# State-space stage of a hybrid decoder: later transposes and Toeplitz products, gelus half a period later, powers loaded from ScalarE's queue

## The chip, the cores and the metric

The kernel runs on one core of one Trainium2 chip. The metric is the time of one execution in device microseconds (us). The inputs lie in HBM as float32, laid out for the kernel on the host; the whole computation, both layers and the final norm, is one launch.

## What is computed

Two residual layers on a sequence of 512 tokens with 1024 channels. Layer 0 mixes tokens by a grouped diagonal complex state-space model (S5), layer 1 by a gated DeltaNet. The change touches layer 0 alone. Cut to what matters there:

```python
def s5_mixer(h, w_in, lam, log_dt, b, c, d_skip, w_glu, w_out):
    u, z = split(h @ w_in, 2)                  # 512 x 2048 each
    ab = exp(lam * exp(log_dt))                # complex, 128 groups x 64 states
    bb = (ab - 1) / lam * b                    # 128 x 64 x 16
    # per group: x[t] = ab * x[t-1] + bb @ u[t];  y[t] = Re(c @ x[t])
    y = scan_over_512_steps(ab, bb, c, u) + d_skip * u
    y = gelu(y)
    y = y * sigmoid(y @ w_glu)                 # 2048 x 2048
    return (y * silu(z)) @ w_out
```

## The kernel before

Every dense product is made with three matmuls of a float32 split in two parts (`mm3`, lines 91 to 94): ScalarE (ACT) rounds a tile to a high part with a copy (CAST), VectorE (DVE) subtracts it to get the low part, and TensorE (PE) multiplies high by high, high by low and low by high. `split` (line 78) does this for a slab of activations, `get_hi` and `next_lo` (lines 337 to 348) for a weight tile of 128x1024.

The stage around the change has two streams. The first is 40 **units** (`unit`, line 375). A unit is one 128x512 output of a dense product, eight steps of three matmuls. Units 0 to 7 give the second half of u, 8 to 23 give z (through a Silu on ACT), and 24 to 39 multiply the first half of the gelu'd y (`yA`, eight slabs of 128x512) by one half of the gate's weights. `fill(n)` puts the next n steps of that stream into PE's order; `unit_end` copies finished outputs out of PSUM and rounds the weights of the unit after next.

The second stream is the state space itself in 16 **steps** of 8 groups (`Step`). The sequence is folded by four, so that one step is: loads of the powers of ab (`wt`, three DMAs out of the DRAM tile `wd`), of `bB` and of u (`s5_load`); `s5_bl` on DVE makes the folded input matrices from `bB` and `wt`, and `s5_mask` on ACT masks them; `s5_v` on PE multiplies them with u; `s5_rot` and `s5_add` on DVE turn the result by the angles whose sine and cosine ACT makes (`s5_angle`, `s5_sincos`); `s5_scan` is a scan on DVE; `s5_unrot` and `s5_state` on DVE turn back; `s5_y` on PE multiplies by the output matrices that `s5_ca` (DVE) and `s5_cl` (ACT) made. Beside that the step builds a Toeplitz product for what happens inside four tokens: `s5_kin` (a small add on DVE, two masks on ACT), `s5_kt` (four transposes on PE, four copies `tl` on ACT), `s5_out` (eight matmuls on PE into the PSUM tile of `s5_y`, then copies `yb` on ACT and the store of y to DRAM as `yd`). For the first eight steps y is read back into the slabs `part[8 + k]`.

`wd` is written by `s5_params` (line 178): DVE computes the first four powers of ab, and SP stores each as it comes (line 250). All loads and stores of this stage are issued by SyncE (SP), which takes them in order.

The loop over i (lines 609 to 661) interleaves the streams. Under `tc.manual_schedule` PE and DVE run exactly in the order in which the code is written; ACT and SP are ordered by a planner that works with modelled durations and takes the ready instruction that stands earliest in the code. In iteration i the step `prev` is i - 1, `cur` is i and `nxt` is i + 1. One iteration has 16 steps of units, that is two units. Ahead of the loop stand five units (`fill(40)`), the parameters and the first step's `s5_v`. Gelus of the first eight slabs (`gelu_a`, line 350) are written in iteration 9; since ACT is the planner's, it issues each as soon as it holds its slab to be loaded. Unit 24 frees the tiles of h, and its eight steps each split one slab of `yA` beside themselves. After the loop `fill(400)` runs what is left of the units.

After the units, lines 669 to 675 load the other eight slabs of y (`yG`), gelu them and split them into `yBhi` and `yBlo`, which take the place of `yA`'s tiles; then each of 16 gate outputs is finished with that half (`glu_half`), and the output product follows.

Of the kernel before, what the change touches and what calls it, by code (L numbers as in the profile page):

```python
# [10 lines left out]
F32 = mybir.dt.float32  # L11
# [7 lines left out]
P = 128  # L19
# [22 lines left out]
def hybrid_kernel(ctx: ExitStack, tc: tile.TileContext, a, out, dbg=None):  # L42
# [314 lines left out]
    def split_y(k):  # L357
        split(part[8 + k], yA[0][:, k, :], yA[1][:, k, :])
# [3 lines left out]
    def unit_end():  # L362
# [10 lines left out]
        ends.clear()  # L373

    def unit(n):
        if n == 24:
            hB.close()
            yAp = yAx.enter_context(tc.tile_pool(name="yAp", bufs=1, side="right", reuse_waits="tile"))
            yA.extend([yAp.tile([P, 8, T], F32R, name="yAhi"), yAp.tile([P, 8, T], F32R, name="yAlo")])
            split_y(0)  # L380
        ps = psm.tile([P, T], F32, tag="mm", name="ps_mm" if n < 24 else "ps_gh")
        whi, wlo = pairs.pop(n)
        xh, xl = (hhi, hlo) if n < 24 else yA
        for k in range(KT):
            if n == 24 and k < 7:
                split_y(k + 1)
            mm3(ps, whi[:, k * P:(k + 1) * P], wlo[:, k * P:(k + 1) * P], xh[:, k, :], xl[:, k, :],
                k == 0, k == KT - 1)
            if k == 3 and lo_within[0]:
                next_lo()  # L390
            if k < KT - 1:
                yield
        ends.append((n, ps))
        if lo_within[0]:
            unit_end()
        yield
# [41 lines left out]

    def s5_load(i):
        s = steps[i]  # L440
        s.wt = s5.tile([P, 3, 256], F32, tag="wt", name="wt", bufs=1)
        for c in range(3):
            SY.dma_start(s.wt[:, c, :], wd[c].rearrange("j g q n -> (j g) (q n)")[:, 256 * i:256 * i + 256]
                         .unsqueeze(1).to_broadcast([8, 16, 256]))
# [18 lines left out]
    def s5_sincos(s):  # L463
# [3 lines left out]
        S.activation(out=s.kr, in_=s.tau, func=AF.Abs)  # L467
        S.activation(out=s.tc, in_=s.kr, func=AF.Sin, scale=-TWO_PI_LO, bias=hpi_c)

# [122 lines left out]
    get_hi(1)  # L592
    fill(40)
    s5_params()
    s5_quad(0)
    cur = s5_load(0)
    s5_quad_b(0)
# [11 lines left out]
    with tc.manual_schedule(engines={mybir.EngineType.PE, mybir.EngineType.DVE}):  # L609
        for i in range(17):  # L610
            nxt = s5_load(i + 1) if i < 15 else None
            if i in (1, 5, 9):
                s5_quad((i + 3) // 4)
            if prev:
                s5_y(prev)
            if cur:
                s5_rot(cur)
            fill(3)
            if prev:
                s5_kin(prev)  # L620
            if cur:
                s5_add(cur)
                s5_cl(cur)
            fill(1)
            next_lo()
            if prev:
                s5_kt(prev)
            if i == 9:
                gelu_a(range(8))
            if nxt:  # L630
                s5_frac(nxt)
                s5_bl(nxt)
            fill(2)
            if nxt:
# [3 lines left out]
            fill(2)  # L638
            unit_end()
            if prev:  # L640
                s5_out(prev)
            if cur:
                s5_unrot(cur)
            fill(4)
            if nxt:
                s5_sincos(nxt)
                s5_side(nxt)
            if i < 14:
                s5_angle(steps[i + 2])
            if nxt:  # L650
                s5_v(nxt)
# [3 lines left out]
            if nxt:  # L655
                s5_ca(nxt)
            if i in (1, 5, 9):
                s5_quad_b((i + 3) // 4)
            fill(4)
            unit_end()  # L660
            prev, cur = cur, nxt
# [10 lines left out]
    yBlo = yBp.tile([P, 8, T], F32R, name="yBlo")  # L672
    with tc.tile_pool(name="yGp", bufs=1, reuse_waits="tile") as yGp:
        for k in range(8):
            split(load_gelu(8 + k, yGp.tile([P, T], F32, name=f"yG{k}")), yBhi[:, k, :], yBlo[:, k, :])
    def glu_half(m, hf, ps, yh, yl):
# [692 lines left out]
```

## Time and profile before

| | us |
|---|---|
| median of three runs | 1084.86 |
| lowest and highest | 1084.20 and 1087.56 |
| the profiled execution, its own time | 1086.08 |
| span of that execution's trace | 1084.4 |

The profile is of that one execution. Busy times of an engine are sums over its instructions; a matmul's end is modelled, so that what PE really loses is better seen from the starts of its instructions and from its waits. All times in a trace are us from the start of its span. An engine that stands idle is charged to what released it. The bracket at the end of a row gives the idle time ahead of that instruction and the releaser.

### The profile page before, as it was taken

How to read it: one execution, taken by the hardware profiler on the slowest of the kernel's cores; microseconds unless marked ns; L12 is line 12 of the kernel's file. 1: busy time of each engine (PE TensorE's matmuls, PEld its weight loads, DVE VectorE, ACT ScalarE, POOL GpSimd, SP SyncE). 2: the span in 40 equal slices, each digit the busy share in tenths (PEclk: the TensorE clock that was granted, in tenths of full speed). 3: DMA queues.
4: the chain of work that ended last, by engine and by line, in shares of the span. 5: the costliest groups of instructions: out<-in, count | busy, mean ns of one | idle time of the engine just before them, and what ended most of it. 6: DMA issues, size and time to landing. Idle time of an engine off the chain costs nothing. (4 is left out here: it accounts for less than half of the span.)

```text
span 1084.4 us, 15225 instructions
## 1 busy us (share of the span) xinstructions
PE 1041.8 (96%) x5620; PEld 869.5 (80%) x5620; DVE 774.9 (71%) x1246; ACT 599.8 (55%) x1163; POOL 57.5 (5%) x62
## 2 busy tenths in 40 slices
PE   7999999998999989999999999999999999999997
PEld 5887878886888868878899777778888888887887
DVE  5994999998999838666785688679951444556253
ACT  4573799989787564334446566733343655424241
POOL 0100000000000000000001004310020000200000
PEclk9999999998999999999999999999999999999999
DMA  8776666675354268866751342132241001123342
GB/s 300 265 244 200 192 195 197 190 214 168 99 148 126 91 248 313 299 208 225 251 179 57 111 164 78 59 99 96 104 131 60 20 20 39 59 72 110 100 146 78
DMA packets 85628, 161.42 MB, mean 149 GB/s; under 512 B 10417, under 2 KB 44593, under 8 KB 85554
## 3 DMA queue, kind: packets, MB, share of 16 engines
q1 hardware_dynamic: 84546, 157.31, 45.0%
q0 software_dynamic: 1008, 3.15, 1.1%
q8 instruction: 44, 0.72, 0.3%
q14 instruction: 30, 0.25, 0.1%
HBM read 141.67 MB, written 18.74 MB: 148 GB/s over the span
## 5 line engine op out<-in xcount | busy, mean ns | idle before, releaser
L79 ACT CAST whi<-wraw 128x1024 fp32r<-128x1024 f32 (+1 forms) x101 | 99.1, 981 | 175.8 <-PE ps_mm L93 74.9
L80 DVE TENSOR_TENSOR wlo<-wraw,whi 128x1024 fp32r<-128x1024 f32 (+1 forms) x101 | 116.1, 1149 | 92.9 <-ACT whi L79 79.6
L92 PE MATMUL ps_mm<-g_hhi,whi 128*128 128x512 f32 x360 | 148.3, 412 | 0.4 <-ACT whi L79 0.4
L93 PE MATMUL ps_mm<-g_hlo,whi 128*128 128x512 f32 x360 | 147.0, 408 | 0.0
L94 PE MATMUL ps_mm<-g_hhi,wlo 128*128 128x512 f32 x360 | 145.8, 405 | 0.5 <-DVE wlo L80 0.5
L94 PEld LDWEIGHTS ps_mm<-g_hhi,wlo 128*128 128x128 f32 x360 | 67.7, 188 | 14.7 <-DVE wlo L80 1.0
L92 PE MATMUL ps_mm<-hhi,whi 128*128 128x512 f32 x192 | 79.3, 413 | 0.0
L92 PEld LDWEIGHTS ps_mm<-g_hhi,whi 128*128 128x128 f32 x360 | 67.7, 188 | 14.3 <-ACT whi L79 0.8
L93 PEld LDWEIGHTS ps_mm<-g_hlo,whi 128*128 128x128 f32 x360 | 67.8, 188 | 12.6
L94 PE MATMUL ps_mm<-hhi,wlo 128*128 128x512 f32 x192 | 75.8, 395 | 0.0
L93 PE MATMUL ps_mm<-hlo,whi 128*128 128x512 f32 x192 | 75.5, 393 | 0.0
L857 DVE SCALAR_TENSOR_TENSOR ac<-ps_mm,cw,ac 128x509 f32<-128x509 f32 (+2 forms) x87 | 64.7, 744 | 3.6 <-ACT ac L854 2.9
L103 DVE SCALAR_TENSOR_TENSOR adaw<-adaw,cact 128x1024 f32<-128x1024 f32 x48 | 58.8, 1228 | 5.0 <-DMA adaw<-in_adaw_dram 4.9
L92 PE MATMUL ps_gh<-yAhi,whi 128*128 128x512 f32 x128 | 53.8, 420 | 3.6 <-ACT yAhi L79 3.6
L346 DVE TENSOR_TENSOR wlo<-wraw,whi 128x1024 fp32r<-128x1024 f32 x40 | 48.7, 1219 | 10.8 <-ACT whi L340 10.8
L340 ACT CAST whi<-wraw 128x1024 fp32r<-128x1024 f32 x40 | 41.8, 1044 | 24.2 <-issue 7.7
L93 PE MATMUL ps_gh<-yAlo,whi 128*128 128x512 f32 x128 | 51.2, 400 | 1.1 <-DVE yAlo L80 1.1
L94 PE MATMUL ps_g<-yBhi,wlo 128*128 128x512 f32 x128 | 50.1, 391 | 1.4 <-DVE wlo L80 1.4
L93 PE MATMUL ps_g<-yBlo,whi 128*128 128x512 f32 x128 | 50.2, 393 | 1.1 <-DVE yBlo L80 1.1
L92 PE MATMUL ps_g<-yBhi,whi 128*128 128x512 f32 x128 | 50.1, 391 | 1.2 <-ACT yBhi L79 1.2
L94 PE MATMUL ps_gh<-yAhi,wlo 128*128 128x512 f32 x128 | 51.0, 399 | 0.0
L94 PEld LDWEIGHTS ps_mm<-hhi,wlo 128*128 128x128 f32 x192 | 36.4, 190 | 8.2
(343 smaller groups left out, 2535.8 us busy)
## 6 DMA issues: line engine op xcount, KB each, us to landing
adaw<-in_adaw_dram SPq DMA_DIRECT2D x48, 512.0 KB
wraw<-in_wginb_dram SPq DMA_DIRECT2D x45, 512.0 KB
wraw<-in_wglu_dram SPq DMA_DIRECT2D x32, 512.0 KB
wraw<-in_winb_dram SPq DMA_DIRECT2D x24, 512.0 KB
bB<-in_bB_dram SPq DMA_DIRECT2D x16, 384.0 KB
wt<-wd SPq DMA_DIRECT2D x48, 128.0 KB
wraw<-in_s5o_a_dram SPq DMA_DIRECT2D x16, 384.0 KB
wraw<-in_wgo_a_dram SPq DMA_DIRECT2D x16, 384.0 KB
```

The costliest lines, as they stand in the source:

```text
L79: S.copy(hi, src)
L80: V.tensor_tensor(out=lo, in0=src, in1=hi.bitcast(F32), op=ALU.subtract)
L92: TE.matmul(ps, whi, xhi, start=start, stop=False)
L93: TE.matmul(ps, whi, xlo, start=False, stop=False)
L94: TE.matmul(ps, wlo, xhi, start=False, stop=stop)
L103: return V.scalar_tensor_tensor(out=aw, in0=aw, scalar=1.0, in1=cact, op0=ALU.mult, op1=ALU.mult, accum_out=mods[:, n:n + 1]).ins
L340: S.copy(pairs[n][0], raws[n])
L346: V.tensor_tensor(out=lo, in0=raws.pop(n), in1=hi.bitcast(F32), op=ALU.subtract)
L857: V.scalar_tensor_tensor(out=ac[:, d:], in0=ps[:, 0:T - d], scalar=cw[:, n, k:k + 1], in1=ac[:, d:], op0=ALU.mult, op1=ALU.add)
```

## The change

- The powers of the first step are loaded by three DMAs that ACT issues and no longer SP. The other steps keep SP.
- Four units and no longer five stand ahead of the loop (`fill(32)`). One unit more is left for the end.
- Within an iteration the transposes (`s5_kt`) move from behind the fourth step of units to behind the sixth, and the Toeplitz products (`s5_out`) from behind the eighth to behind the tenth. `s5_y`, `s5_v` and `unit_end` stay where they are, at 0, 12, 8 and 16 steps.
- The gelus of the first eight slabs are queued on ACT behind the sine and cosine of step 10 (in iteration 9). `s5_v` of that step moves to the end of iteration 9, ahead of unit 24, which now begins with iteration 10. The first two slabs of `yA` are split at the end of iteration 9, the other six beside the first three steps of unit 24.
- The loads for the last four steps' tables (`s5_quad`, `s5_quad_b`) move from iteration 9 to 10, and in iteration 10 the small add of `s5_kin` stands ahead of the first units.
- After the units, the loads and gelus of the other eight slabs are written in a loop of their own with a higher priority for the planner, and the splits follow in a second loop.

```diff
--- before.py
+++ after.py
@@ -372,18 +372,21 @@
             get_hi(n + 2)
         ends.clear()
 
+    def start_half():
+        hB.close()
+        yAp = yAx.enter_context(tc.tile_pool(name="yAp", bufs=1, side="right", reuse_waits="tile"))
+        yA.extend([yAp.tile([P, 8, T], F32R, name="yAhi"), yAp.tile([P, 8, T], F32R, name="yAlo")])
+        split_y(0)
+        split_y(1)
+
     def unit(n):
-        if n == 24:
-            hB.close()
-            yAp = yAx.enter_context(tc.tile_pool(name="yAp", bufs=1, side="right", reuse_waits="tile"))
-            yA.extend([yAp.tile([P, 8, T], F32R, name="yAhi"), yAp.tile([P, 8, T], F32R, name="yAlo")])
-            split_y(0)
         ps = psm.tile([P, T], F32, tag="mm", name="ps_mm" if n < 24 else "ps_gh")
         whi, wlo = pairs.pop(n)
         xh, xl = (hhi, hlo) if n < 24 else yA
         for k in range(KT):
-            if n == 24 and k < 7:
-                split_y(k + 1)
+            if n == 24 and k < 3:
+                split_y(2 * k + 2)
+                split_y(2 * k + 3)
             mm3(ps, whi[:, k * P:(k + 1) * P], wlo[:, k * P:(k + 1) * P], xh[:, k, :], xl[:, k, :],
                 k == 0, k == KT - 1)
             if k == 3 and lo_within[0]:
@@ -436,11 +439,11 @@
                         in1=qT[:, 2:3, ns].unsqueeze(3).to_broadcast([P, 2, 16, 16]), op=ALU.mult)
         V.tensor_tensor(out=bb, in0=ys[0], in1=ys[1], op=ALU.subtract)
 
-    def s5_load(i):
+    def s5_load(i, q=SY):
         s = steps[i]
         s.wt = s5.tile([P, 3, 256], F32, tag="wt", name="wt", bufs=1)
         for c in range(3):
-            SY.dma_start(s.wt[:, c, :], wd[c].rearrange("j g q n -> (j g) (q n)")[:, 256 * i:256 * i + 256]
+            q.dma_start(s.wt[:, c, :], wd[c].rearrange("j g q n -> (j g) (q n)")[:, 256 * i:256 * i + 256]
                          .unsqueeze(1).to_broadcast([8, 16, 256]))
         s.bB = s5.tile([P, 3, 256], F32, tag="bB", name="bB")
         SY.dma_start(s.bB, a["bB"].rearrange("p (c n) -> p c n", c=3)[:, :, 256 * i:256 * i + 256])
@@ -465,7 +468,7 @@
         s.ts = s5.tile([P, 4, P], F32, tag="tsin", name="tsin")
         S.activation(out=s.ts, in_=s.tau, func=AF.Sin, scale=-TWO_PI_LO)
         S.activation(out=s.kr, in_=s.tau, func=AF.Abs)
-        S.activation(out=s.tc, in_=s.kr, func=AF.Sin, scale=-TWO_PI_LO, bias=hpi_c)
+        return S.activation(out=s.tc, in_=s.kr, func=AF.Sin, scale=-TWO_PI_LO, bias=hpi_c).ins
 
     def s5_side(s):
         qs = slice(4 * s.i, 4 * s.i + 4)
@@ -590,10 +593,10 @@
     get_hi(0)
     next_lo()
     get_hi(1)
-    fill(40)
+    fill(32)
     s5_params()
     s5_quad(0)
-    cur = s5_load(0)
+    cur = s5_load(0, S)
     s5_quad_b(0)
     s5_bl(cur)
     s5_mask(cur)
@@ -609,54 +612,60 @@
     with tc.manual_schedule(engines={mybir.EngineType.PE, mybir.EngineType.DVE}):
         for i in range(17):
             nxt = s5_load(i + 1) if i < 15 else None
-            if i in (1, 5, 9):
+            if i in (1, 5, 10):
                 s5_quad((i + 3) // 4)
             if prev:
                 s5_y(prev)
             if cur:
                 s5_rot(cur)
+            if prev and i == 10:
+                s5_kin(prev)
             fill(3)
-            if prev:
+            if prev and i != 10:
                 s5_kin(prev)
             if cur:
                 s5_add(cur)
                 s5_cl(cur)
-            fill(1)
             next_lo()
-            if prev:
-                s5_kt(prev)
-            if i == 9:
-                gelu_a(range(8))
             if nxt:
                 s5_frac(nxt)
                 s5_bl(nxt)
-            fill(2)
+            fill(3)
+            if prev:
+                s5_kt(prev)
             if nxt:
                 s5_mask(nxt)
             if cur:
                 s5_scan(cur)
             fill(2)
             unit_end()
+            fill(2)
             if prev:
                 s5_out(prev)
             if cur:
                 s5_unrot(cur)
-            fill(4)
+            fill(2)
             if nxt:
-                s5_sincos(nxt)
+                last = s5_sincos(nxt)
                 s5_side(nxt)
+            if i == 9:
+                with tc.issue_after(last):
+                    gelu_a(range(8))
             if i < 14:
                 s5_angle(steps[i + 2])
-            if nxt:
+            if nxt and i != 9:
                 s5_v(nxt)
             if cur:
                 s5_state(cur)
             next_lo()
             if nxt:
                 s5_ca(nxt)
-            if i in (1, 5, 9):
+            if i in (1, 5, 10):
                 s5_quad_b((i + 3) // 4)
             fill(4)
+            if i == 9:
+                s5_v(nxt)
+                start_half()
             unit_end()
             prev, cur = cur, nxt
         lo_within[0] = True
@@ -671,8 +680,13 @@
     yBhi = yBp.tile([P, 8, T], F32R, name="yBhi")
     yBlo = yBp.tile([P, 8, T], F32R, name="yBlo")
     with tc.tile_pool(name="yGp", bufs=1, reuse_waits="tile") as yGp:
+        yG = []
         for k in range(8):
-            split(load_gelu(8 + k, yGp.tile([P, T], F32, name=f"yG{k}")), yBhi[:, k, :], yBlo[:, k, :])
+            with tc.high_priority(600):
+                yG.append(load_gelu(8 + k, yGp.tile([P, T], F32, name=f"yG{k}")))
+        for k in range(8):
+            split(yG[k], yBhi[:, k, :], yBlo[:, k, :])
+
     def glu_half(m, hf, ps, yh, yl):
         whi, wlo = load_w(a["wglu"][2 * m + hf])
         for k in range(8):
```

## Rows read from the trace of the kernel before

**Rows 1.** Page, part 1: busy us (share of span) and instructions.
```profile
PE 1041.8 (96%) x5620; PEld 869.5 (80%) x5620; DVE 774.9 (71%) x1246; ACT 599.8 (55%) x1163; POOL 57.5 (5%) x62
```

**Rows 2.** Waits of PE, 66 to 362 us: total, times, longest.
```profile
PE ps_kt L566 <- ACT kin L560: 4.4, 4, 2.3
PE ps_y L574 <- ACT tl L569: 3.8, 4, 1.8
PE ps_v L514 <- ACT bl L487: 3.6, 2, 2.6
PE ps_gh L92 <- ACT yAhi L79: 3.6, 1, 3.6
```

**Rows 3.** Windows: length, busy PE, PEld, DVE, ACT, POOL; clock, DMA.
```profile
66.50:93.70 27.20, 27.20 (x121) 22.33 (x119) 18.53 (x52) 13.47 (x24) 0.00 (x0) 1.00 0.75 237
99.90:253.00 153.10, 143.68 (x790) 121.29 (x790) 150.76 (x194) 132.34 (x242) 0.00 (x0) 0.99 0.67 198
...
279.00:362.10 83.10, 82.81 (x469) 71.01 (x468) 81.63 (x106) 61.11 (x122) 0.00 (x0) 1.00 0.43 121
...
395.80:407.00 11.20, 8.36 (x30) 5.13 (x30) 8.69 (x14) 10.16 (x19) 0.00 (x0) 1.00 0.86 326
```

**Rows 4.** Waits of DVE, 99 to 362.1 us.
```profile
DVE za L523 <- PE ps_v L514: 4.9, 1, 4.9
DVE kc L558 <- PE ps_y L550: 3.0, 4, 1.3
DVE yAlo L80 <- ACT yAhi L79: 0.5, 1, 0.5
```

**Rows 5.** Timeline of DVE: start, us; first rotation of steps 0, 14 and 15.
```profile
99.94 1.23 DVE L523 TENSOR_TENSOR za<-ps_v,tcos 128x1024 f32<-128x1024 f32 x1 [4.89 <-PE ps_v L514]
...
345.65 1.22 DVE L523 TENSOR_TENSOR za<-ps_v,tcos 128x1024 f32<-128x1024 f32 x1
...
362.13 1.22 DVE L523 TENSOR_TENSOR za<-ps_v,tcos 128x1024 f32<-128x1024 f32 x1
```

**Rows 6.** Timeline of PE: v of step 0 (first matmuls) and step 15.
```profile
96.47 0.65 PE L514 MATMUL ps_v<-U,bl 128*128 128x128 f32 x3 [2.59 <-ACT bl L487]
...
357.19 1.95 PE L514 MATMUL ps_v<-U,bl 128*128 128x128 f32 x16
```

**Rows 7.** Timeline of SP's issues, 81 to 87 us.
```profile
81.64 0.86 SPq L250 DMA_DIRECT2D wd<-p  x2
82.59 0.68 SPq L443 DMA_DIRECT2D wt<-wd  x1
...
85.10 0.61 SPq L443 DMA_DIRECT2D wt<-wd  x1
...
86.26 0.43 SPq L75 DMA_DIRECT2D wraw<-in_winb_dram  x1
86.78 0.60 SPq L443 DMA_DIRECT2D wt<-wd  x1
```

**Rows 8.** Timeline of DVE, 86 to 94 us: first readers of the powers.
```profile
86.59 0.69 DVE L479 TENSOR_TENSOR ta<-bB,wt 128x512 f32<-128x512 f32 x1 [1.07 <-DMA wt<-wd]
...
93.63 0.69 DVE L480 TENSOR_TENSOR tb<-bB,wt 128x512 f32<-128x512 f32 x1 [3.02 <-DMA wt<-wd]
```

**Rows 9.** Groups of ACT, 100 to 280 us: table loads ahead of gelus.
```profile
L352 ACT ACT_TABLE_LOAD x8 | 10.3, 1283 | 0.1
```

**Rows 10.** Timeline of ACT, 351 to 358 us: iteration 14.
```profile
351.16 0.63 ACT L466 ACTIVATE tsin<-tau 128x512 f32<-128x512 f32 x1 [1.45 <-DVE tau L461]
351.70 1.69 ACT L569 COPY tl<-ps_kt 32x512 f32<-32x512 f32 x4
...
357.26 0.74 ACT L468 ACTIVATE tcos<-kr,cols 128x512 f32<-128x512 f32 x1
```

**Rows 11.** Timeline of ACT, 393 to 394.4 us: two gelus of 128x512.
```profile
393.13 1.15 ACT L585 ACTIVATE yG<-yG 128x512 f32<-128x512 f32 x2
```

**Rows 12.** Waits of PE, 395 to 407 us.
```profile
PE ps_g L92 <- ACT yBhi L79: 1.2, 1, 1.2
```

## The prediction

> **What bounds the kernel now.** I read the page first: PE is busy for 96% of the span, DVE for 71% [rows 1]. That reads as a kernel bound by PE, in which a wait of PE that goes is time won. The waits of PE in the state-space stage name what the change aims at: 4.4 us for the masked `kin` ahead of the transposes, 3.8 for the `tl` copies ahead of the Toeplitz products, 3.6 for `bl` ahead of `s5_v`, 3.6 for the first slab of `yA` [rows 2]. But a share over the whole span mixes stages, so the windows came next. From 99.9 to 253.0 us DVE is busy for 150.76 of 153.10 us, and from 279.0 to 362.1 for 81.63 of 83.10 [rows 3]. In the loop it is DVE that never rests. The waits of DVE confirm it: in 262 us it waits 3.0 us for `ps_y` and 0.5 for the split of `yA`; the 4.9 for `ps_v` lie ahead of its first rotation at 99.94 [rows 4, 5]. One period late in the loop, from rotation 14 to rotation 15, is 362.13 - 345.65 = 16.48 us [rows 5].
>
> So the loop from rotation 0 to rotation 15 lasts 262.2 us, of which 262.2 - 3.5 = 258.7 are work of DVE that the change neither adds to nor takes from. PE's work in a period is a little less, so PE falls idle now and then wherever its order first meets something that DVE has not begun yet: a kin, a tl (which waits behind a sine on ACT that waits for DVE's `tau` [rows 10]), a state. Most of the waits in [rows 2] are this lag becoming visible. Moving PE's instruction later hides the wait there and shows it elsewhere. The reader is to see that the end of the stage is: the start of rotation 0, plus DVE's loop, minus what PE may run ahead of DVE at the end, plus PE's work after that.
>
> **The change part by part.** I work out the four terms of that sum, against the profiled execution (1086.08 us, span 1084.4; 1.2 us above the median).
>
> Start of the loop. A unit is 24 matmuls; 121 of them take 27.20 us [rows 3], 0.225 each, 5.4 us a unit. With four units ahead, PE reaches the first `s5_v` 5.4 us earlier than now, near 88, and does that unit after the loop, where nothing hides it: +5.4. In return `s5_v` has to come earlier. It starts at 96.47 [rows 6]; its last input is the third power load, which DVE's reader took at 93.63 [rows 8], 2.84 us before. SP issued the three loads at 82.59, 85.10 and 86.78, the last behind a 512 KB weight load at 86.26 [rows 7]. The second waited for the stores of the powers, the last two of which began at 81.64 [rows 7]: no queue can start it before 85.10. On ACT, the second and third start at 85.10 and 85.71. The first load took 4.0 us from its issue to its reader (82.59 to 86.59), the third 6.85 (86.78 to 93.63) [rows 7, 8]. A load that ACT issues is not in this trace, so I bound it: 3.0 us as a floor (a store, at the second of the two, from about 82.07 to its reader at 85.10), 6.85 as the ceiling. I take 4.0, the load with no weights right ahead of it, as ACT's queue has none: landed at 89.7, `s5_v` at 92.55, 3.9 us earlier than now. Net +1.5 (bounds +0.5 and +4.4). ACT's issues themselves hold it for three times 0.6 us; it is busy for 13.47 of 27.20 us there [rows 3], so I cost them at nothing; without that cover they would push a weight cast by 1.8 us, and PE is waiting then anyway.
>
> DVE's idle time inside the loop, 3.5 us now. The wait for `ps_y` goes, as it comes from PE being held up by ACT in iterations 7 to 9: each early gelu brings a table load of 1.28 us, eight of them [rows 9], and one back, and waits for its slab, ahead of the `tl` copies. Behind the sine and cosine one load serves all eight. In their place comes one block: in iteration 14 the last cosine starts at 357.26 and takes 0.74, so ends at 358.0, 4.1 us before DVE is through (362.13) [rows 5, 10]; the later Toeplitz product moves both by the same. From there ACT needs 1.28 for the table, 8 gelus at 1.15 / 2 [rows 11] = 4.6, and 0.6 for the first cast, of a gelu's size: 6.5. DVE, which is to subtract next, idles 2.4. That is -1.1 (bounds: 0 idle, -3.5; and 6.2 idle, +2.7, if ACT also serves another table load, 1.28, a Silu like a gelu, 0.6, and some 2 us of weight cast and kin before the third slab).
>
> How far PE may run ahead. Now `s5_v` of step 15 starts at 357.19 and its rotation at 362.13, 4.94 later [rows 5, 6]. The limit is the `tl` chain; both it and the product that needs it move by two steps, six matmuls, 1.36 us. So the lag at the end may grow by that: -1.4 (bounds 0, if the state for the next `s5_y` binds at once, and -2.0). This is all that the shift of transposes and products brings, however many waits it hides.
>
> The second half of y. From 395.8 to 407.0 PE has 30 matmuls in 11.20 us, worth 6.8 [rows 3]: 4.4 lost while ACT alternates gelus and casts. With the gelus done early, what stays is the first cast, which can't start before unit 39 has read the tile it overwrites, 1.2 [rows 12], and the first subtraction, near 0.6, half of a 1.22 us operation on twice the columns [rows 5]: -2.6 (bounds -3.4 and 0, where the loads come too late). The work that hides the gelus is the unit left for the end.
>
> Sum: +1.5 - 1.1 - 1.4 - 2.6 = -3.6. The profiled execution would take 1082.5; set against the median, 1084.86 - 3.6 = **1081.3 us**. Nothing after 407 us changes.
>
> **The rivals.**
>
> (A) The second queue saves only issue time. The third load then still needs its 6.85 us, from 85.71: `s5_v` at 95.4, the shift costs +4.4, the sum is -0.7 and the time 1084.2. For it: DMA was busy 75% of the time just before, at 237 GB/s [rows 3], and the first load may have been quick because it was alone. Against it: the third stood right behind 512 KB on the same queue [rows 7]. The Trainium skill, in "DMA: Bandwidth & Descriptors", section "Issuing engines are not separate DMA queues", says that starting DMAs from several engines saves only the sequencer's time to start them, since all run on the same 16 engines; by that rule this rival holds. The same page, section "Queues, rings and completion order", has each DMA engine take turns between queues, by which a load on another queue need not sit out the 512 KB; no row here shows two hardware queues at once.
>
> (B) Slower: ACT reaches its three triggers late. ACT takes them in order, and where the planner puts them behind the cast that waits for the end of the fourth unit, near 88 (66.5 and four units of 5.4), they start near 89.9 with that cast and its copy done (an estimate: three gelus of 0.57 [rows 11], by their columns), the third 1.2 later, and it lands at 95.1, `s5_v` at 98; with the slow 6.85 at 100.8. The shift then costs +6.9 to +9.7 and the sum is +1.8 to +4.6, 1086.7 to 1089.5. From `s5_v` at 96.2 on the kernel is no faster than before, from 99.5 on it is slower by 0.3%. For it: the planner's modelled time need not be the chip's. Against it: on SP it put the first loads near 82.6 and 85, in good time [rows 7].
>
> (C) The waits are real. Every wait of [rows 2] and the 1.2 of [rows 12] go, 16.6 us: 1068.3. Against it stands DVE's 258.7 us of work, which would have to begin 14.5 us earlier (the 16.6, less the 3.5, 1.4 and 2.6 that the other terms can give, plus the unit's 5.4) [rows 4, 5].
>
> (D) The block of gelus costs its ceiling of 6.2 us of DVE's time, the rest as forecast: +3.8, so 1085.1. For it: casts, Silu and copies all meet there.
>
> **How the numbers follow.** The forecast has 0.53, A 0.22, B 0.13, C 0.03, D 0.09. The range takes in A and D and most of B, and the better bounds of each term (-0.9 at the start, -2.4 of idle, -0.6 of lag, -0.8 at the second half; two of the larger together): 1076 to 1088. A measurement of this kernel can tell 0.3%, 3.3 us, from no change. The forecast lies just past that: of its 0.53 some 0.43 fall beyond it, with C and a share of the early landings of A's kind 0.50 in all; within it 0.36, from the rest of the forecast, A and D; slower 0.14, B and the worst of D.
>
> **What would show it.** In the changed profile: DVE busy for 98% from rotation 0 to 15 and the period still 16.5 us; rotation 0 near 96 and not 94 or 100; `s5_v` of step 0 with a longer wait than 2.59; one gelu table load in the loop and a DVE wait for `yAhi` of some 2.4 us; rotation 15 some 6.3 us after the start of its `s5_v`; PE waits for kin and tl that shrink early and come back, at y, tl or kt, late in the loop; ps_g with one wait of 1.2. Wrong would be a period below 16.4, a first power load on ACT that takes over 6 us, or PE with no waits in the loop at all.

## The result, and the profile after

The changed kernel takes **1097.58 us** (median of 6 runs, 1093.12 to 1098.42) against 1084.53 for the kernel before on the same chip (6 runs): a ratio of **1.0097** with a 95% interval of 1.0075 to 1.0120 (the quotient of the two medians, 1.0120, is the upper end of that interval). Forecast were 1081.3 us and, with a chance of 0.14, a slower kernel. The profiled execution took 1093.12 us with a span of 1091.4, the quickest of the six; against the profiled execution of before it is 7.0 us longer.

The first part of the page of the changed kernel (busy us, share of the span, instructions):

```profile
PE 1045.0 (96%) x5620; PEld 871.9 (80%) x5620; DVE 774.4 (71%) x1246; ACT 583.1 (53%) x1148; POOL 57.6 (5%) x62
```

The shares are those of before [rows 1]: ACT has lost 15 instructions and 16.7 us. All 15 are table loads: one gelu load in the loop where there were eight [rows 9], and eight fewer of the other tables. The kernel is no faster for it. The waits of PE in the changed kernel, from 66 to 362 us (total, times, longest):

```profile
PE ps_v L517 <- ACT bl L490: 10.3, 9, 4.0
PE ps_gh L92 <- ACT yAhi L79: 3.6, 2, 2.3
PE ps_kt L569 <- ACT kin L563: 2.3, 2, 1.6
PE ps_y L577 <- ACT tl L572: 2.0, 3, 0.9
```

The waits for kin and tl have halved, as the change meant, and the wait for `bl` has grown from 3.6 to 10.3 [rows 2]: the sum went from 15.4 to 18.2 us. A wait that is only a sign of an engine behind moves when the instruction is moved. The stretches that answer to [rows 3] (length, busy PE, PEld, DVE, ACT, POOL; clock, DMA) and the waits of DVE inside the loop:

```profile
98.90:252.00 153.10, 144.93 (x808) 122.89 (x807) 151.39 (x194) 115.00 (x226) 0.00 (x0) 0.99 0.65 200
278.00:361.40 83.40, 80.44 (x449) 68.70 (x448) 82.50 (x107) 63.02 (x125) 0.00 (x0) 0.98 0.43 120
...
DVE yAlo L80 <- ACT yAhi L79: 4.2, 4, 3.1
```

DVE is busy for 99% of both stretches and now has a single cause of waiting. Its 3.0 us for `ps_y` [rows 4] are gone, 3.7 more for the split of `yA` have come. The timeline of DVE (start, us) at rotations 0, 14 and 15, and of PE at `s5_v` of steps 0 and 15:

```profile
98.95 1.23 DVE L526 TENSOR_TENSOR za<-ps_v,tcos 128x1024 f32<-128x1024 f32 x1 [5.24 <-PE ps_v L517]
344.92 1.22 DVE L526 TENSOR_TENSOR za<-ps_v,tcos 128x1024 f32<-128x1024 f32 x1
361.40 1.22 DVE L526 TENSOR_TENSOR za<-ps_v,tcos 128x1024 f32<-128x1024 f32 x1
...
95.13 0.58 PE L517 MATMUL ps_v<-U,bl 128*128 128x128 f32 x1 [4.04 <-ACT bl L490]
355.10 1.16 PE L517 MATMUL ps_v<-U,bl 128*128 128x128 f32 x9
```

Against [rows 5, 6]: rotation 0 comes 1.0 earlier, the loop lasts 262.45 in place of 262.19, the period is 16.48 in both, and the lag from `s5_v` of step 15 to its rotation grew from 4.94 to 6.30.

The table follows these marks (us, starts of single instructions) through all kernels of this study. "Units" is the last product of unit 39, "out" the first of the output projection, "solves" the stretch from the first small matmul of the first layer's solves (`ps_m`) to the product that follows them (`ps_pq`); the last column is the time against before, run on the same chip in the same set, with its interval. before-2 is the kernel before once more.

| kernel | v(0) | rot 0 | rot 15 | lag | units | units to out | solves | ratio |
|---|---|---|---|---|---|---|---|---|
| before | 96.47 | 99.94 | 362.13 | 4.94 | 395.53 | 15.92 | 56.8 | 1 |
| before-2 | 95.58 | 97.66 | 360.23 | 4.93 | 393.64 | 15.94 | 56.7 | 1.0003 (0.9988 to 1.0018) |
| **after** | 95.13 | 98.95 | 361.40 | 6.30 | 398.88 | 16.46 | 59.7 | 1.0097 (1.0075 to 1.0120) |
| a1 | 95.89 | 99.36 | 361.80 | 6.30 | 399.28 | 17.64 | 59.7 | 1.0071 (1.0043 to 1.0099) |
| b2 | 95.80 | 99.62 | 360.05 | 4.93 | 398.89 | 13.08 | 61.3 | 1.0024 (1.0002 to 1.0045) |
| b3 | 96.34 | 99.84 | 361.14 | 4.96 | 394.52 | 15.93 | 56.7 | 1.0009 (0.9996 to 1.0023) |
| b4 | 94.86 | 96.95 | 359.85 | 5.02 | 393.20 | 18.54 | 61.3 | 1.0052 (1.0030 to 1.0073) |
| b5 | 95.14 | 97.23 | 358.99 | 4.97 | 397.80 | 13.60 | 56.7 | 1.0023 (1.0004 to 1.0041) |
| c1 | 96.65 | 100.33 | 360.06 | 3.96 | 394.44 | 15.95 | 61.3 | 1.0005 (0.9985 to 1.0024) |
| a2 | 94.89 | 98.71 | 361.11 | 6.29 | 398.62 | 14.82 | 59.7 | 1.0047 (1.0031 to 1.0063) |
| a3 | 96.50 | 100.32 | 362.72 | 4.94 | 401.56 | 15.40 | 59.7 | 1.0070 (1.0049 to 1.0091) |
| a4 | 94.97 | 98.37 | 357.78 | 6.30 | 395.29 | 18.26 | 59.7 | 1.0062 (1.0038 to 1.0086) |
| d1 | 94.77 | 96.86 | 361.97 | 4.94 | 395.36 | 16.25 | 59.8 | 1.0029 (1.0014 to 1.0044) |
| d2 | 96.25 | 100.07 | 362.49 | 6.30 | 399.99 | 14.96 | 56.7 | 1.0076 (1.0047 to 1.0106) |

Of the 7.0 us of the profiled executions, 3.35 are there when the units end, 3.9 when the output projection begins, 4.3 when the solves begin, and 7.2 behind them. One pair of traces is a thin base, since the start of the loop differs by 2.3 us between before and before-2. The means of two traces each (before and before-2, after and a1) put the changed kernel 4.5 us behind at the end of the units, 5.6 at the output projection, 6.5 at the start of the solves and 9.4 behind them.

### The profile page after: what moved, and what is told of

Same layout as the page of the kernel before. It is cut to its first block, busy times and chain, and to the rows that moved or that the text cites. A ratio compares the mean times of both kernels' runs of the same rounds, so it can differ in the third digit from the quotient of the medians.

```text
span 1091.4 us, 15229 instructions
## 1 busy us (share of the span) xinstructions
PE 1045.0 (96%) x5620; PEld 871.9 (80%) x5620; DVE 774.4 (71%) x1246; ACT 583.1 (53%) x1148; POOL 57.6 (5%) x62
## 5 line engine op out<-in xcount | busy, mean ns | idle before, releaser
L80 DVE TENSOR_TENSOR wlo<-wraw,whi 128x1024 fp32r<-128x1024 f32 (+1 forms) x101 | 116.1, 1150 | 94.8 <-ACT whi L79 81.6
```

The source lines that it names most:

```text
L80: V.tensor_tensor(out=lo, in0=src, in1=hi.bitcast(F32), op=ALU.subtract)
```

## The experiments

**The changed kernel again (a1).** No edit.

> The changed kernel unaltered, for its spread and a second trace. Theory 1 (the loss lies in the state-space stage: one unit of 5.4 us more behind a loop that is bound by VectorE and starts only 1.0 us earlier): the first matmul of the second half of the gate product comes some 4 us later than before, in every trace. Theory 2 (the loss is mostly the clock): TensorE's granted clock falls below 0.97 between 830 and 840 us, in the triangular solves of layer 1, for some 3 us, and this run repeats that and shows at which other place the time goes up to the median of 1097.6.

Ratio 1.0071; together with the first measurement the change costs some 0.7 to 1.0%. The marks up to the units repeat: loop 262.44, lag 6.30, units at 399.28. The solves take 59.7 us again. So both theories have their mark, and what is lost is lost in the same places, with 1.2 us more from the units to the output projection, at a granted clock of 0.90 there (1.00 in the first trace).

**One unit less ahead, and the loads on ACT's queue (b2), in the kernel before.**

```diff
-    fill(40)
+    fill(32)
-    cur = s5_load(0)
+    cur = s5_load(0, S)
```
(with `q.dma_start` for the three loads of `s5_load`, as in the change)

> The kernel before with four units ahead of the loop and the first step's powers on ScalarE's queue, nothing else. Theory 1: the unit costs 5.4 us and the start of the loop gives back 1.0 to 1.3, so +4.1 to +4.4 at the first matmul of the second half, and the whole kernel +4 to +5. Theory 2: the same +4 there, and the clock in layer 1 decides the rest: +4 where it doesn't fall, +7 where it does. Rival (the two parts are harmless, the gelus and the shift cost the time): within 1 us.

The units end at 398.89, 3.4 later than before: PE's tail from `s5_v` of step 15 to there is 43.78 us against 38.34, one unit (5.44). Ahead of the loop next to nothing came back: rotation 0 at 99.62 is 0.3 earlier than in before and 2.0 later than in before-2; the loop itself is 1.8 shorter (260.43). But the output projection begins 13.08 after that and not 15.92, at 411.97 against 411.45. The unit covers the gelus of the second half, by 2.8 us. In this kernel, without the rest of the change, the term that I had put at -2.6 is there. The whole kernel loses some 2.6 us (1.0024), less than theory 1 had.

**The queue alone (b3).** The same edit of `s5_load`, with `fill(40)`.

> Before, with one part of the change alone: the three power loads of step 0 go on ScalarE's queue; the number of units ahead of the state-space stage stays as in before. Theory (the loads come about 1 us earlier by the issue alone, their flight hardly changes): first s5_v at 95.1 to 95.5, rotation 0 near 98.9, the last product of the units about 1.0 earlier, near 394.5, and a time 1 us below the one of before, so between 0.998 and 1.000 of it. Rival (the second queue removes the transfer behind the weights): first s5_v near 92.6, rotation 0 near 96, the end 3.5 us earlier.

Neither time came. `s5_v` starts at 96.34. The issues of ACT and the first readers of the loads on DVE in this kernel (the second row holds the second and third issue, the third row the third alone, from a window of the timeline that begins between them):

```profile
81.85 1.17 ACTq L443 DMA_DIRECT2D wt<-wd  x1
...
84.78 1.29 ACTq L443 DMA_DIRECT2D wt<-wd  x2
...
85.49 0.58 ACTq L443 DMA_DIRECT2D wt<-wd  x1
...
86.88 0.69 DVE L479 TENSOR_TENSOR ta<-bB,wt 128x512 f32<-128x512 f32 x1 [1.45 <-DMA wt<-wd]
93.50 0.69 DVE L480 TENSOR_TENSOR tb<-bB,wt 128x512 f32<-128x512 f32 x1 [5.93 <-DMA wt<-wd]
```

The third load started 1.3 us earlier than in before (85.49 against 86.78) and its reader ran 0.13 earlier (93.50 against 93.63): 8.0 us from issue to reader in place of 6.85 [rows 7, 8]. The ratio is 1.0009, with 1 in its interval: no gain. In d1, which has the same edit, the third load took 6.7 us.

**One unit of work more (b5), in the kernel before.** The 24 products of unit 39 are made twice, the first pass overwritten; nothing is left out.

```diff
+        for k in range(8 if n == 39 else 0):
+            mm3(ps, whi[:, k * P:(k + 1) * P], wlo[:, k * P:(k + 1) * P], xh[:, k, :], xl[:, k, :],
+                k == 0, k == 8 - 1)
         for k in range(KT):
```

> The kernel before with the 24 matmuls of its last unit made twice (the first pass is overwritten), so that all that follows is 5.4 us later and nothing else is changed. Theory 1: +5.4 at the first matmul of the second half, and no more after it. Theory 2: +5.4 there, and the clock may fall in the solves of layer 1 at some 830 us, since they begin at another moment: then +8 to +9 at the end.

The tail is 43.78, again 5.44 longer, and the output projection begins 13.60 after it: the second half hides 2.3 of the 5.4. Started at 97.23, near the 97.66 of before-2, it reaches the output projection at 411.40 against 409.58. So a unit of work more costs less than its length in this kernel, but not nothing.

**The shift of transposes and products alone (b4), in the kernel before.**

```diff
-            fill(1)
             next_lo()
-            if prev:
-                s5_kt(prev)
...
-            fill(2)
+            fill(3)
+            if prev:
+                s5_kt(prev)
...
             unit_end()
+            fill(2)
             if prev:
                 s5_out(prev)
             if cur:
                 s5_unrot(cur)
-            fill(4)
+            fill(2)
```

> The kernel before with the transposes and the Toeplitz products two steps later, nothing else. Theory 1 with the lag of the prediction: rotation 15 comes 6.3 us after the start of its matmuls in place of 4.94, so the end of the units 1.4 us earlier; the kernel -1.4. Rival (the waits hidden are time won): the waits for kin and tl, 8.2 us, go and the kernel is 5 us or more faster.

Neither time came: the kernel is slower, by 0.5%. The lag stayed at 5.02. One row of the windows, from 340 to 358 us, first of this kernel and then of the changed one, bears on why:

```profile
340.00:358.00 18.00, 17.92 (x101) 15.22 (x100) 17.83 (x24) 12.41 (x24) 0.00 (x0) 1.00 0.31 91
```
```profile
340.00:358.00 18.00, 17.47 (x99) 14.88 (x98) 17.79 (x24) 13.30 (x27) 0.00 (x0) 1.00 0.36 100
```

Here PE is busy without a gap (17.92 of 18.00), so a later product gives it nothing to run ahead into. In the changed kernel it waits now and then, so it is as far ahead as the order lets it be. That is how I read the two rows; no run tests it by itself. The shift alone also puts the last Toeplitz product, and with it the last store of y, 1.4 us nearer to the end of the units (10.2 ahead of it in place of 11.6). The first cast of the second half then holds PE for 4.4 us, and the output projection begins 18.54 after the units. Part of that is the clock, which falls behind this wait:

```profile
393.20:411.70 18.50, 14.14 (x50) 10.85 (x49) 12.73 (x20) 14.92 (x25) 0.00 (x0) 0.82 0.91 327
```

At 0.82, a fifth of the stretch is lost (18.5 x 0.18 = 3.3 us).

**The change without its shift (a3).** `s5_kt` and `s5_out` back at their places of before.

> The changed kernel with the transposes and Toeplitz products where they were before. Theory 1 (the shift lets TensorE run 1.36 us further ahead of VectorE): rotation 15 comes 4.94 us after the start of its matmuls in place of 6.30, the units end 1.4 us later, the last store of y is 1.4 us earlier against their end; on the whole within 1.5 us of the changed kernel. Rival (the shift costs time by itself, as the kernel before with the shift alone was 5 us slower): 3 to 5 us faster than the changed kernel.

The lag is 4.94: in the changed kernel the shift is what makes it 6.30. With that the units end 1.36 later relative to rotation 15 (38.84 against 37.48). From there to the output projection it is 15.40 against 16.46, at a granted clock of 0.89 in that stretch (1.00 in the changed kernel), which is worth some 1.7 us of it. So what the shift wins at the end of the loop it pays back right behind. The ratio, 1.0070, is that of a1, as theory 1 had it.

**The change with the second half of y written as before (a2).** One loop of load, gelu and split, no raised priority.

> The changed kernel with the loads, gelus and splits of the second half in one loop again and no raised priority, as before the change. Theory 1b (the new order of that part costs time: the loads stand behind a weight load on SyncE's queue that waits for VectorE, and ScalarE makes all eight gelus before the first cast): from the last matmul of the units to the first of the layer's first projection of layer 1 it takes 180.4 us as with the kernel before plus fill(32) and ScalarE's queue (180.36), in place of 183.8; the kernel is 3.4 us faster than the changed one. Rival (order there makes no difference): within 1 us of the changed kernel.

From the units to the output projection 14.82 us in place of 16.46, both at a granted clock of 1.00, and the ratio falls to 1.0047, below the interval of the first measurement but inside that of a1. Up to that mark the new loop loses 1.6 us. At the mark that the expectation named, the first product of layer 1's first projection, nothing of it is left in the trace: 184.05 us from the units to there, 183.81 in the changed kernel, where 180.4 was forecast. The stretch of the output projection took 1.9 us longer in this trace (169.23 against 167.35), for which I have no cause.

**The change with the early gelus free to go when the planner likes (a4).**

```diff
-                with tc.issue_after(last):
-                    gelu_a(range(8))
+                gelu_a(range(8))
```

> The changed kernel with the gelus of the first eight slabs not queued behind the sine and cosine of step 10, so that the planner places them. Theory 1 (VectorE's 258 us of work bound the loop, and table loads on ScalarE cost only what they make VectorE wait): eight table loads of 1.28 us for gelus come back, VectorE's waits for yAhi (4.2 us) shrink to 1, and the time from rotation 0 to rotation 15 stays between 259 and 262.5 us. Rival (the waits of TensorE for tl are time won by the block): the loop gets 3 us or more longer.

The loop takes 259.41 us, 3.0 less, and DVE waits 1.4 for `yAlo` and not 4.2:

```profile
DVE yAlo L80 <- ACT yAhi L79: 1.4, 2, 1.0
```

So the block of gelus behind the cosine costs 3 us of DVE's time, as theory 1 had it. The units end 3.6 earlier than in the changed kernel. Half of that was gone when the output projection began (413.55 against 415.34), since that stretch took 18.26 us, with PE waiting 3.1 for the first cast and 1.5 for a weight, and at a granted clock of 0.91. A ratio of 1.0062 can't be told from the 1.0071 of a1.

**A little less work for DVE (c1), in the kernel before.** One subtraction of each step, 0.69 us, goes to GpSimd.

```diff
-        V.tensor_tensor(out=xs, in0=xs, in1=xt, op=ALU.subtract)
+        G.tensor_tensor(out=xs, in0=xs, in1=xt, op=ALU.subtract)
```

> The kernel before with one operation a step, the last subtraction of the output matrices (128x512, 0.69 us on VectorE), on GpSimd. Theory 1 (VectorE bounds the loop): each period gets 0.6 us shorter, 15 of them 9 us, until TensorE's own work of some 16.2 us a period binds; the end of the units 5 to 9 us earlier, the kernel 5 to 9 us faster. Rival (TensorE's waits are latencies of its own): the period stays at 16.4 or more and the time within 2 us. Second rival (GpSimd and VectorE slow each other down): VectorE's operations beside it take longer than the 0.68 to 1.22 us of before.

The loop shortens by 2.5 us, not by the 9 that 15 times 0.6 would give. Three early periods lose the whole 0.7 (15.70 to 15.76 us, 16.43 to 16.48 in before), others grow, and the last four are 16.06 to 16.32. PE's waits do not vanish, and DVE now waits for PE (from rotation 0 to 15):

```profile
DVE kc L558 <- PE ps_y L550: 5.0, 11, 0.8
```

Late in the loop PE's own work stands 0.2 to 0.4 us a period behind DVE's. The second rival falls: DVE's other operations keep their 0.68 to 1.22 us beside GpSimd's 1.33. That DVE bounds the loop was right; that it alone does was not.

**The kernel before again (b0).** No edit.

> The kernel before, unaltered, for a second trace of it. Theory: the fall of the granted clock during the solves of the first layer (56.8 us in the trace of before, 59.7 in the changed kernel, 61.3 in three variants) belongs to the execution, not to the code: then this trace may show 59 to 62 us between the start of the solves and the step after them, with everything up to there within 1 us of the first trace, and a longer span by as much. Rival: it belongs to the kernel, and this trace shows 56.8 again. Time 1084 to 1088 either way; first s5_v near 96.5, rotation 0 near 99.9, the last product of the units at 395.5.

56.7 us for the solves again, as the rival had it, and a rotation 0 at 97.66: the start of the loop varies by 2.3 us between two executions of the same kernel.

**The loads of the second half on GpSimd's queue (d1, before with b3's edit; d2, the changed kernel).**

```diff
-        SY.dma_start(yr, yd[k])
+        G.dma_start(yr, yd[k])
```
(in `load_gelu`)

> Before, with the power loads of step 0 on ScalarE's queue and the eight loads of the second half of y on GpSimd's queue (idle there) in place of SyncE's. Theory: these eight loads wait on SyncE's queue behind a weight load whose buffer is not free, not for their own data; on GpSimd's queue they start by 11 us before the last product of the units (7.0 before it in the kernel before), the gelus follow earlier, and the output projection begins about 13 us after that product in place of 15.9: with the queue at the start 3 to 4 us in all, so 0.996 to 0.998 of before. Rival: the loads are bound by the landing of the last store of y, or GpSimd issues them more slowly than SyncE does: then they land no earlier and the output projection stays at 15 to 16 us after the product; time 0.998 to 1.002 of before.

> The changed kernel with the eight loads of the second half of y on GpSimd's queue. Theory: the part of the prediction that failed here (2.6 us were to be won in the second half of y) failed through the place of these loads behind a weight load on SyncE's queue; on a queue of their own they start 12 us or more before the last product of the units (7.9 in the changed kernel), all gelus are done by its end, and the output projection begins 13 to 14 us after it in place of 16.5: 2.5 to 3.4 us less than the changed kernel, so a ratio to before near 1.004 to 1.006. Rival: what binds there is the order of the work on ScalarE and VectorE (casts, subtractions, the weights of the next unit); then the loads come earlier and the output projection stays at 16 to 17.5 us after the product.

In d1 the loads start early, and nothing follows from it. GpSimd's issues, the first six of the eight, and ACT's rows some 30 us later show the reason:

```profile
361.92 3.42 POOL L584 DMA_DIRECT2D yG<-yd  x6 [302.45 <-DMA yd<-yb]
...
392.54 1.28 ACT L724 ACT_TABLE_LOAD   x1 [0.88 <-DMA yr<-yd]
393.84 0.63 ACT L724 ACTIVATE yr<-yr 128x512 f32<-128x512 f32 x1
394.37 1.14 ACT L585 ACTIVATE yG<-yG 128x512 f32<-128x512 f32 x2
```

In before, SP issues all eight from 388.53 on. But ACT takes another gelu first and waits for that one's load, so the first gelu of `yG` runs at 394.37, 1.24 later than in before [rows 11], and gelus and casts alternate as they did. The output projection begins 16.25 after the units, at a granted clock of 0.90 there (1.00 in before), so that this figure alone decides nothing. The casts do: the first starts 0.9 behind the last product of the units and the eighth 7.67, in before 0.9 and 7.69. The theory fell: in before it is the order of ACT's work that binds, not the place of the loads. In d2, where all gelus are written ahead of the casts, earlier loads do help: the first gelus start 7.84 before the last product of the units in place of 2.39, PE's wait of 1.8 for the next unit's weight goes, and the output projection begins 14.96 after it, 1.5 earlier. The wait for the first cast stays (2.8). Against before d2 is at 1.0076, not better than the changed kernel by anything that can be measured.

## Why the prediction was wrong

The frame held. Start of rotation 0, DVE's loop, the lag and PE's tail add up to the end of the units, and on to the output projection, in every kernel of the table. Up to that projection I had forecast -3.6 us; it was +3.9 (5.6 by the means of two traces each). Term by term, for the profiled pair:

**Start of the loop: forecast +1.5, measured +4.5.** This step and the second half of y failed most, by some 3 us each. The unit that is no longer ahead came back in the tail as 5.44 us, the 5.4 of [rows 3]. `s5_v` came 1.34 earlier and not 3.9, and rotation 0 came 0.99 earlier. Even that is within what the start varies by. Over the table, `s5_v` starts at 95.7 on average with five units ahead (seven traces, 94.8 to 96.6) and at 95.6 with four (seven, 94.9 to 96.5): the change gave back nothing there. Rotation 0 comes 0.9 later with four units (99.3 against 98.4), and PE's wait ahead of `s5_v`, longer with four, is followed by a clock of 0.50 to 0.58 in all seven of those traces and in three of the others (the last section has the figures). By these means the start costs 5.4 + 0.9 = 6.3. ACT issued on time. The issues on ACT in the changed kernel, and the readers:

```profile
82.76 1.17 ACTq L446 DMA_DIRECT2D wt<-wd  x1
85.49 1.29 ACTq L446 DMA_DIRECT2D wt<-wd  x2
...
87.81 0.69 DVE L482 TENSOR_TENSOR ta<-bB,wt 128x512 f32<-128x512 f32 x1 [1.48 <-DMA wt<-wd]
92.29 0.69 DVE L483 TENSOR_TENSOR tb<-bB,wt 128x512 f32<-128x512 f32 x1 [3.79 <-DMA wt<-wd]
```

I had taken 4.0 us from issue to reader. The first took 5.05. The third, issued at about 86.2 (0.71 behind the second, as in b3), took 6.1, and in b3 8.0: a queue without weights ahead of it did not make it short. Over all traces the third load took 5.5 to 6.9 us from SP's queue (five traces) and 6.1 to 8.0 from ACT's (nine), and its reader ran at 92.9 and 92.8 on average. This is close to rival A. That its `s5_v` at 95.4 and its +4.4 for the start (its own working gives +4.3) agree with the profiled trace (95.13 and +4.45) is in part luck: the trace that the forecast was made from started late, and A's gain of 1.1 us is not there on average. Between 4.0 and 6.85 I had chosen the better end, on the ground that the slow load stood behind 512 KB on its queue; that ground was wrong.

What the third load waited for stands in the DMA packets. ACT's loads ride a hardware queue of their own (q10), 136 packets each. In the changed kernel the 272 packets of the first two end at 89.80 us. Those of the third, issued at 86.2, run from 89.90 to 91.82, and its reader starts 0.5 later. The two queues from 89.85 to 92 us (packets, MB, share of 16 engines; q1 is SP's):

```profile
q1 hardware_dynamic: 335, 0.38, 49.3%
q10 hardware_dynamic: 136, 0.13, 17.3%
```

So 3.7 of the 6.1 us passed until the second load was through, with SP's data moving beside it, and 1.9 were its own transfer. In the other eight traces with ACT's queue the third load's packets, counted in order, begin within 0.5 us of the end of the second's. My 4.0 us were those of a load with none of the three ahead of it; the second load, 0.6 ahead on the same queue, stood in my sum at nothing. No run gave the three loads different queues.

The Trainium skill, "DMA: Bandwidth & Descriptors", section "Issuing engines are not separate DMA queues", says that a second issuing engine saves only the time to start the transfers. The traces here agree that no more than that is saved: the third load's reader ran 1.3 us earlier in the changed kernel and 0.1 in b3, and on average over all traces 0.1.

**DVE's idle time in the loop: forecast -1.1, measured +0.3.** The wait for `ps_y` went, as forecast, but not for my reason. It is gone in a4 too, where the eight gelu loads are back; and in before 2.1 of its 3.0 us stand in iteration 9 (256.6 to 257.6 us), the rest in 5 and 10. What a3, a4 and the changed kernel share, and before, b2 and b4 lack, is the new order around iterations 9 and 10, with unit 24 begun later; no run tests that alone. (I had also left out 0.3 us that DVE waits for a weight.) The block cost 4.2 in place of 2.4. ACT's timeline around it in the changed kernel:

```profile
262.74 0.75 ACT L471 ACTIVATE tcos<-kr,cols 128x512 f32<-128x512 f32 x1
263.49 1.28 ACT L352 ACT_TABLE_LOAD   x1
264.78 4.27 ACT L352 ACTIVATE p<-p 128x512 f32<-128x512 f32 x8
268.96 1.26 ACT L460 ACTIVATE tau<-cst,t 128x128 f32<-128x128 f32 x4
270.13 0.60 ACT L79 CAST yAhi<-p 128x512 fp32r<-128x512 f32 x1
```

The table load and the gelus are near what I had (1.28 and 4.3, for 1.28 and 4.6). Missing from my sum is `s5_angle`, which stands ahead of the first cast: 1.26 us for four `tau`. Behind it come another table load and a `z` ahead of the third cast, the ceiling of rival D, of which only small waits came (0.44, 0.21, 0.54). a4 shows the whole block at 3.0 us.

**Lag: forecast -1.4, measured -1.36.** Right, with a condition that I had not stated: PE must have waits to lose. Without the rest of the change it brings nothing (b4, lag 5.02).

**Second half of y: forecast -2.6, measured +0.5.** The argument was right for the unit alone (b2: -2.8). Two other parts of the change took it back. By the stretches at a granted clock of 1.00, from the units to the output projection: b2 13.08, the shift with the old loop 14.82 (a2), the shift with the new loop 16.46 (the changed kernel). In this order the shift took back 1.7 and the new loop 1.6. In the other order the shares differ: a3, the new loop without the shift, needs 15.40 at a clock of 0.89, some 13.7 at 1.00 (an estimate, as above), so the new loop costs most of its part only together with the shift. The shift stores the last step's y 1.36 us nearer to the units' end (the last Toeplitz product 15.64 us ahead of it, 17.0 in b2), and SP's loads then stand behind a weight load. The rows of SP in the changed kernel, and the waits of PE from 395 to 418 us:

```profile
385.10 1.96 SPq L582 DMA_DIRECT2D yd<-yb  x4
390.54 0.35 SPq L75 DMA_DIRECT2D wraw<-in_wglu_dram  x1
390.94 3.77 SPq L587 DMA_DIRECT2D yG<-yd  x8
...
PE ps_g L92 <- ACT yBhi L79: 2.5, 1, 2.5
PE ps_g L94 <- DVE wlo L80: 1.8, 1, 1.8
PE ps_g L93 <- DVE yBlo L80: 0.2, 1, 0.2
```

The first gelu starts 2.39 us before the last product, so the eight are not done when the tile comes free, and the first cast comes 2.26 after that product (0.90 in before). The raised priority puts the eighth gelu ahead of it, and all eight casts and subtractions ahead of the next unit's weight: hence the 1.8, which my sum did not have. In all 4.5 us of waits stand where 4.4 were lost before [rows 3]. What failed is a sentence of the prediction: "The work that hides the gelus is the unit left for the end" held only where the loads were early enough (b2), and I had not followed the step's store through the queue.

**"Nothing after 407 us changes": it did.** From the output projection to the solves the changed kernel lost 0.4 us, and in the solves 2.9. The windows over them (before, changed, b4, d2):

```profile
800.60:857.40 56.80, 56.80 (x666) 47.04 (x666) 16.65 (x24) 26.85 (x55) 0.00 (x0) 1.00 0.15 48
```
```profile
804.90:864.60 59.70, 59.70 (x666) 49.20 (x666) 16.63 (x24) 26.87 (x55) 0.00 (x0) 0.94 0.14 45
```
```profile
802.70:864.00 61.30, 61.30 (x666) 50.35 (x666) 16.64 (x24) 26.84 (x55) 0.00 (x0) 0.92 0.14 44
```
```profile
805.20:862.00 56.80, 56.80 (x667) 47.10 (x667) 16.73 (x24) 26.86 (x55) 0.00 (x0) 1.00 0.16 48
```

The same 666 matmuls (667 in d2) take 56.8, 59.7 or 61.3 us by the granted clock (1.00, 0.94, 0.92). d2 has all of the change and 56.8, c1 has none of it and 61.3, so this is no price of one edit. It may still belong to the program as a whole and not to the execution: the two kernels that were traced twice gave the same length twice (56.8 and 56.7, 59.7 and 59.7). Over all executions the clock is lower in the changed kernel: on average 0.987 and 0.988 in its two sets of runs against 0.990 to 0.991 in three sets of before. At 1090 us a mean of 0.003 is 3.3 us at most, a third to two fifths of what the change costs (7.7 us in the set of a1, 10.5 in the first). It is likely less: among the 75 executions of before in those sets, whose clocks go from 0.986 to 0.995, a clock lower by 0.003 goes with 1 to 2 us. And a2 has the mean clock of before in its set (0.991) and takes 5 us more. So most of the loss is likely the terms above. Why the clock falls more often with this change is open: five of its six traces (after, a1 to a4) fall in the solves, and none of the four traces of before, b0, b3 and b5 does, but b2, b4, c1 and d1 do.

No kernel tried is faster than before. b0, b3 and c1 can't be told from it.

## What to carry to other kernels

When two engines run a loop in lockstep, the waits of the one are where its lag shows; count what the change adds to the stretch that no loop covers, here a unit of 5.44 us, before counting the waits it hides. A term that rests on a transfer that the trace does not show belongs at the slow end of its bounds: moving a small load to another queue moved its issue and not its landing. Where a stall is to be hidden by other work, follow each input of the stalled step, its store, its load and what stands ahead of both on their queue, at the new place.

## What the runs showed of the hardware

A wait of PE can cost more than its length. Behind its wait of 4.04 us ahead of `s5_v` of step 0 the changed kernel has a granted clock of 0.50 (the level of 1.2 GHz) from 95 to 100 us, and its rotation 0 comes 3.82 after `s5_v`; before-2, with a wait of 1.28, keeps 1.00 (2.4 GHz) and needs 2.09. The other traces go with these: waits of 1.26 to 1.69 there kept 1.00 and the 2.09 (four traces), and waits of 2.59 to 5.50 were followed by 0.50 to 0.58 up to rotation 0, which came 3.40 to 3.82 behind `s5_v` (ten traces, all seven with four units ahead among them). The two rows, changed kernel first:

```profile
95.00:100.00 5.00, 4.87 (x20) 4.58 (x21) 1.05 (x1) 0.08 (x1) 0.00 (x0) 0.50 0.57 169
```
```profile
95.00:100.00 5.00, 4.42 (x27) 3.96 (x28) 2.34 (x2) 1.94 (x3) 0.00 (x0) 1.00 0.46 140
```

In the solves it fell although PE was busy throughout by the profile, on the same 666 matmuls (512 of them of 32x32 or 64x64) on which it did not fall in other traces.
